# Scan stage of a three-layer network on one core: 32x32 blocks of two chunks inverted at once, every second row on a partition, transfers in two pieces instead of four

## The chip, the cores and the metric

The kernel runs on one core of one Trainium2 chip. The metric is the device time of one execution in microseconds, the median of several runs. One launch computes the whole network; its weights and inputs lie in the chip's memory in float32.

## What is computed

The network has a gated linear recurrence layer, an RWKV-7 layer and an S5 layer, for 1024 tokens of width 1024. The change lies in the RWKV-7 layer's scan, which has 16 heads of 64 channels and, in the reference, goes token by token:

```python
def step(S, inp):
    r_t, w_t, k_t, v_t, a_t, b_t = inp
    sa = jnp.einsum('bhvk,bhk->bhv', S, a_t)
    S = S * w_t[:, :, None, :] + sa[..., None] * b_t[:, :, None, :] + v_t[..., None] * k_t[:, :, None, :]
    y = jnp.einsum('bhvk,bhk->bhv', S, r_t)
    return S, y
```

The kernel does it in 16 chunks of 64 tokens. Inside a chunk, the tokens depend on each other through a 64x64 lower triangular matrix per head, and what the state receives needs the inverse of it (unit diagonal).

## The kernel before

`rwkv_scan` writes the scan as coroutines. Each yields, ahead of every piece of work, the engine that does it, a guessed duration and the events that it waits for. `weave_` takes those coroutines, together with the ones of the dense part (`rwkv_dense`: the projections of the layer) and of the output projection (`rwkv_out`), and lays down one fixed order for each engine: at each step it takes the piece that can start first by its guesses. On the chip each engine then goes through its own list in order. So a piece that stands late in a list runs late, whatever is free.

The dense part comes in four segments of 256 tokens, so four chunks can be scanned after each segment. For chunk c the scan does:

- `load_q` brings the tile QT (three buffers, `NAM` = 3; the load for chunk c waits until chunk c-3 is done, event `("y", c - 3, ..)`). `inner` multiplies it with BK (one buffer, reloaded for the second half of the heads) and DVE masks the products into AM (L1146; three buffers too).
- `diagonal` stores the two 32x32 diagonal blocks of each head to memory (abD, L1166), and `blocks` loads them into GB (L1175) as 32 (head, block) pairs on 32 partitions. It does so four times, once for each group of 32 partitions.
- `inverse` inverts all 32 blocks of the chunk by substitution on DVE: 31 steps, each a multiplication into TB (L1188) and an addition into YB (L1191) that needs it. Group e of 32 partitions holds rows e, e+4, e+8, ... of the inverse, so a step s works on s//4+1 rows of 31-s columns. YB starts as a copy of `eye`. Two chunks are in work at once, in two buffers of GB and YB; the last two chunks have buffers of their own.
- `inverted` stores YB (yiD, L1199) and `whole` loads it into YF (L1210), transposes on DVE (XT, L1215) and computes the off-diagonal block with two small matmuls (L1221, L1231) and copies on ACT (WL, YF).
- `turned` turns V and BK by TensorE; `chain` makes R from AM, QT and the state (L1286, L1289, ACT copy), multiplies it with the inverse YF (L1297; ACT copies it to UV, L1300), and updates the state St (L1306, DVE). The next chunk's `chain` needs that state.
- `outs` makes the chunk's output y (L1329, L1333; ACT copies it to PY, L1336, which sets the event `("y", c, h)`), and `post` normalizes it (L1346 with `cen`, L1477 and L1483 on psq), and `outputs` stores it to outD (event `("out", c)`).

`rwkv_out` multiplies outD with a weight matrix for tokens 0 to 511 and, as its second part, 512 to 767. Its matmuls read the tiles XO, which its coroutine `operands` makes from loads of outD (XR, L1418). It loads three tiles ahead of the one that it splits, in one sequence through both parts. The first part waits for `("out", 7)` and the end of the dense part, the second for `("out", 11)`:

```python
ks = [(y, k) for y in range(len(parts)) for k in range(KD)]
for x in range(len(ks) + nr):
    if x < len(ks):
        (y, k), (t0, n, wait) = ks[x], parts[ks[x][0]]
        yield E("S", 1, 1.46 * n / HT, wait=(list(wait) if k == 0 else []) + ...
```

Of the kernel before, what the change touches and what calls it, by code (L numbers as in the profile page):

```python
# [11 lines left out]
ALU = mybir.AluOpType  # L12
PSUM = bass.MemoryType.PSUM

P = 128
# [9 lines left out]
ILAT = 0.13  # L25
# [31 lines left out]
class Net:  # L57
# [1025 lines left out]
    def rwkv_scan(self):  # L1083

        nc, E = self.nc, self.step
        ch3 = lambda t: t.rearrange("p (c t) -> p c t", t=64)
        rsl = [slice(0, 64), slice(64, 128)]
        NC = 16
# [3 lines left out]
        two = lambda tag, shape, n=2: [self.tiny(f"{tag}{i}", shape, 1) for i in range(n)]  # L1092

        NT, NG = NC - TAIL[0], NC - TAIL[1]

        def slots(tag, shape, n, N, zero=False):
            first = dict(enumerate(two(tag, shape, n))) if tag != "AM" else {}
            last = {}
            for x in first.values() if zero else ():
                nc.gpsimd.memset(x, 0.0)  # L1100

            def get(c):
                if c < N:
                    if c % n not in first:
                        first[c] = self.tiny(f"{tag}{c}", shape, 1)
                    return first[c % n]
                if c not in last:
                    last[c] = self.rtop.tile(list(shape), F32, tag=f"{tag}t{c}", name=self.n(tag), bufs=1)
                    if zero:
                        nc.gpsimd.memset(last[c], 0.0)  # L1110
                return last[c]

            return get

        YF = slots("YF", (P, 8, 64), 2, NG, True)
        QT, AM = slots("QT", (P, 8, 2, 64), NAM, NT), slots("AM", (P, 8, 2, 2, 64), NAM, NT)
        G, Y = slots("GB", (P, 32, 32), 2, NG), slots("YB", (P, 8, 32), 2, NG)
        UV, BT, PY = two("UV", (P, 8, 2, 64)), two("BT", (P, 8, 2, 64), 1), two("PY", (P, HT))
        own = lambda c: ["rtop"] if c >= min(NT, NG) else []

        eye = self.tiny("eye", (P, 8, 32), 1)
        nc.gpsimd.memset(eye, 0.0)
        for e in range(4):
            r = eye[32 * e : 32 * e + 32]
            nc.gpsimd.affine_select(out=r, in_=r, compare_op=ALU.not_equal, fill=1.0, base=-e,
                                    pattern=[[-4, 8], [1, 32]], channel_multiplier=0)
        mask = self.msk.rearrange("p a b -> p (a b)").unsqueeze(1).to_broadcast([P, 4, 128])
        D, O = {}, {}

# [21 lines left out]
        def load_bk():  # L1151
            for x in range(2 * NC):
                c, j0 = x // 2, x % 2 * 4
                yield E("S", 1, 0.73, wait=ready(c, j0, j0 + 4) + ([("bf", x - NBK)] if x >= NBK else []), sig=[("bk", x)], par=True)
                BK[x] = self.tiny("BK", (P, 4, 2, 64), NBK)
                nc.sync.dma_start(BK[x], self.bkD[c][:, j0 : j0 + 4])
# [12 lines left out]

        def blocks():  # L1170
            for c in range(NC):
                yield E("S", 4, 1.46, wait=[("ab", c)] + ([("sub", c - 2)] if 2 <= c < NG else own(c)), sig=[("in", c)], par=True)
                src = D.pop(c).rearrange("h x j s t -> (h x j) s t")
                for e in range(4):
                    nc.sync.dma_start(G(c)[32 * e : 32 * e + 32], src)  # L1175

        def inverse(q):

            for c in range(q, NG, 2) if q < 2 else [q]:
                yield E("G", 0.97, wait=[("in", c)] + ([("yd", c - 2)] if 2 <= c < NG else own(c)))  # L1180
                g, y = G(c), Y(c)
                nc.gpsimd.tensor_copy(y, eye)
                for s in range(31):
                    nj, n = s // 4 + 1, 31 - s
                    us = 0.07 + nj * n / 960
                    yield E("V", us, lat=ILAT)
                    w = self.tiny(f"TB{q % 4}", (P, 80), 2)[:, 0 : nj * n].rearrange("p (j t) -> p j t", t=n)
                    nc.vector.tensor_mul(w, y[:, 0:nj, s : s + 1].to_broadcast([P, nj, n]),  # L1188
                                         g[:, s : s + 1, s + 1 :].to_broadcast([P, nj, n]))
                    yield E("V", us, lat=ILAT, sig=[("sub", c)] if s == 30 else ())  # L1190
                    nc.vector.tensor_add(y[:, 0:nj, s + 1 :], y[:, 0:nj, s + 1 :], w)  # L1191

        def inverted():
            for c in range(NC):
                yield E("S", 4, 0.73, wait=[("sub", c)], sig=[("yd", c)], par=True)
                yD = self.dram.tile([2, 2, 8, 32, 32], F32, name=self.n("yiD"))
                ye = yD.rearrange("h x j (k e) t -> e (h x j) k t", e=4)
                for e in range(4):
                    nc.sync.dma_start(ye[e], Y(c)[32 * e : 32 * e + 32])  # L1199
                D[c, 1] = yD  # L1200

        def whole():
# [67 lines left out]
        def chain(h):  # L1270

            js = slice(4 * h, 4 * h + 4)
            Eb = lambda e: self.EdA[:, js, e : e + 1].to_broadcast([P, 4, 64])
            state = lambda: self.tiny(f"St{h}", (P, 4, 64), 3)
            for c in range(NC):
                am, bt, uv, qz, yf = AM(c), BT[0], UV[c % 2], QT(c), YF(c)
                first = c == 0
                s = st[h][c]
                if c and c % per == 0:
                    yield E("V", 0.32, wait=ready(c))  # L1280
                    nc.vector.tensor_mul(s, s, Eb(5 * (c // per) + 4))
# [12 lines left out]
                u = ch3(ch)[:, 4:8]  # L1294
                for x in range(4):
                    for rs in rsl:
                        nc.tensor.matmul(u[rs, x], yf[rs, 4 * h + x], R[rs, x], start=True, stop=True)  # L1297
                yield E("A", 0.52)
                for hd, rs in enumerate(rsl):
                    nc.scalar.copy(uv[rs, js, 1 - hd, :], u[rs])  # L1300
                if c + 1 < NC:
                    yield E("P", 0.62, wait=[("bt", c, h)], use=0.8)
                    sp = ch3(ch)[:, 0:4]
                    for x in range(4):
                        for hd, rs in enumerate(rsl):
                            nc.tensor.matmul(sp[rs, x], bt[:, 4 * h + x, hd, :], uv[:, 4 * h + x, hd, :],  # L1306
                                             start=True, stop=True)
                    n, e = None, 5 * (c // per) + c % per
                    if not first:
                        yield E("V", 0.34, rel=ch)  # L1310
                        n = self.tiny(f"R{h}", (P, 4, 64), 1)
                        nc.vector.tensor_add(n, sp, s)
                    yield E("V", 0.32, rel=ch if first else None, wait=[("y", c - 2, h)] if c >= 2 else [],
                            sig=[("S", c, h)])
                    st[h][c + 1] = state()
                    nc.vector.tensor_mul(st[h][c + 1], sp if first else n, Eb(e))
                else:
                    yield E("P", 0.0, rel=ch, sig=[("S", c, h)])
# [54 lines left out]
        def outputs():  # L1373
            for c in range(NC):
                yield E("S", 1, 1.46, wait=[("o", c)], sig=[("out", c)], par=True)
                nc.sync.dma_start(self.outD[:, :, 64 * c : 64 * c + 64].rearrange("j p t -> p j t"), O[c % 2])

        return ([chain(0), chain(1), outs(0), outs(1), whole(), [inverse(q) for q in [0, 1, *range(NG, NC)]], blocks(), turned(), [inner(), load_bk()], diagonal(),
                 inverted(), load_q(), post(), outputs()])

    def reopen(self, wait, sig, right):
# [952 lines left out]
```

## Time and profile before

| | us |
|---|---|
| median of 3 runs | 4096.43 (4092.74 to 4096.48) |
| the profiled execution's own time | 4097.04 |
| its span, first to last instruction | 4095.0 |
| busy in the span: PE / DVE / ACT / POOL | 3826.3 / 2530.0 / 1472.3 / 184.2 |

PE is TensorE's matmuls, PEld its weight loads, DVE VectorE, ACT ScalarE, POOL GpSimd, SP the engine that issues most transfers. A time "at 2111 us" is counted from the start of the span. The RWKV-7 stage that the change touches runs from about 1300 to 2303 us; the scan of the first chunk begins at about 1550 us.

### The profile page before, as it was taken

How to read it: one execution, taken by the hardware profiler on the slowest of the kernel's cores; microseconds unless marked ns; L12 is line 12 of the kernel's file. 1: busy time of each engine (PE TensorE's matmuls, PEld its weight loads, DVE VectorE, ACT ScalarE, POOL GpSimd, SP SyncE). 2: the span in 40 equal slices, each digit the busy share in tenths (PEclk: the TensorE clock that was granted, in tenths of full speed). 3: DMA queues.
4: the chain of work that ended last, by engine and by line, in shares of the span. 5: the costliest groups of instructions: out<-in, count | busy, mean ns of one | idle time of the engine just before them, and what ended most of it. 6: DMA issues, size and time to landing. Idle time of an engine off the chain costs nothing.

```text
span 4095.0 us, 57944 instructions
## 1 busy us (share of the span) xinstructions
PE 3826.3 (93%) x22238; PEld 3151.6 (77%) x22238; DVE 2530.0 (62%) x5213; ACT 1472.3 (36%) x2507; POOL 184.2 (4%) x374
## 2 busy tenths in 40 slices
PE   7998999999999888898979699999999999999899
PEld 6776788888877778787867677888887787888687
DVE  6565733333363688788766584444437699997655
ACT  5456411111132675555543321121114323323523
POOL 0000000000000010000010010011100000000000
PEclk8999999999999899999989799999999999999999
DMA  3111111111122699678776522121212244343775
GB/s 110 47 44 44 56 42 52 42 57 42 45 63 80 203 256 253 171 212 213 205 201 180 151 75 66 44 68 52 72 36 63 75 127 117 107 121 102 234 226 190
DMA packets 688548, 464.97 MB, mean 114 GB/s; under 512 B 189652, under 2 KB 609424, under 8 KB 688272
## 3 DMA queue, kind: packets, MB, share of 16 engines
q1 hardware_dynamic: 515376, 370.42, 30.7%
q10 hardware_dynamic: 167552, 81.80, 7.1%
q0 software_dynamic: 5344, 9.05, 0.7%
q8 instruction: 175, 2.87, 0.3%
q14 instruction: 101, 0.83, 0.1%
HBM read 355.11 MB, written 107.22 MB: 113 GB/s over the span
## 4 chain that ended last, share of the span: by engine, by line
PE 62%; DVE 16%; DMA 8%; issue 7%; ACT 5%; POOL 1%; SPq 1%; ACTq 0%; DVEq 0%; POOLq 0%
PE mm L249 14%; PE mm L251 14%; PE mm L250 13%; PE ob L249 4%; PE ob L250 4%; PE ob L251 4%; DVE cy L1928 4%; DMA wraw<-in_rw_w_rkv_dram 1%; DVE w L881 1%; PE mm L2119 1%; DVE w L216 1%; PE mm L2118 1%; PE mm L2117 1%; DMA GB<-abD 1%; DVE TB L1188 1%
## 5 line engine op out<-in xcount | busy, mean ns | idle before, releaser
L249 PE MATMUL mm<-T,w 128*128 128x512 f32 (+1 forms) x2944 | 1152.2, 393 | 49.6 <-ACT w L215 26.7
L251 PE MATMUL mm<-T,w 128*128 128x512 f32 (+1 forms) x2944 | 1148.0, 391 | 4.6 <-DVE w L216 4.6
L250 PE MATMUL mm<-T,w 128*128 128x512 f32 (+1 forms) x2944 | 1149.9, 391 | 1.0 <-DVE T L1426 0.9
L249 PEld LDWEIGHTS mm<-T,w 128*128 128x128 f32 x2944 | 558.3, 190 | 176.2 <-ACT w L215 31.0
L251 PEld LDWEIGHTS mm<-T,w 128*128 128x128 f32 x2944 | 558.5, 190 | 121.5 <-DVE w L216 6.4
L250 PEld LDWEIGHTS mm<-T,w 128*128 128x128 f32 x2944 | 559.2, 190 | 116.0 <-DVE T L1426 1.6
L215 ACT CAST w<-wraw 128x1024 fp32r<-128x1024 f32 (+1 forms) x286 | 288.3, 1015 | 991.8 <-PE mm L250 695.5
L216 DVE TENSOR_TENSOR w<-wraw,w 128x1024 fp32r<-128x1024 f32 (+1 forms) x286 | 335.1, 1177 | 373.4 <-ACT w L215 371.4
L396 DVE TENSOR_TENSOR h<-ob,h 128x512 f32<-128x512 f32 x416 | 286.3, 690 | 233.5 <-PE ob L251 230.1
L249 PE MATMUL ob<-S,w 128*128 128x512 f32 x896 | 360.3, 402 | 22.1 <-DVE h L396 21.2
L1928 DVE SCALAR_TENSOR_TENSOR cy<-cu,pv,cy 128x512 f32<-128x512 f32 x480 | 350.8, 748 | 12.3 <-ACT cy L1926 2.6
L251 PE MATMUL ob<-S,w 128*128 128x512 f32 x896 | 355.6, 397 | 0.0
L250 PE MATMUL ob<-S,w 128*128 128x512 f32 x896 | 355.2, 396 | 0.0
L249 PE MATMUL mm<-M,w 128*128 128x256 f32 x768 | 259.5, 338 | 18.9 <-ACT M L855 11.0
L250 PE MATMUL mm<-N,w 128*128 128x256 f32 x768 | 229.7, 299 | 12.2 <-DVE N L857 12.2
L251 PE MATMUL mm<-M,w 128*128 128x256 f32 x768 | 229.6, 299 | 5.7 <-DVE w L881 5.4
L249 PEld LDWEIGHTS ob<-S,w 128*128 128x128 f32 x896 | 170.3, 190 | 71.3 <-DVE h L396 30.6
L251 PEld LDWEIGHTS ob<-S,w 128*128 128x128 f32 x896 | 170.3, 190 | 39.0
L250 PEld LDWEIGHTS ob<-S,w 128*128 128x128 f32 x896 | 170.6, 190 | 36.4 <-DVE S L216 0.4
L446 DVE TENSOR_TENSOR S<-mm,S 128x512 f32<-128x512 f32 x88 | 60.8, 691 | 211.2 <-PE mm L251 209.4
L249 PEld LDWEIGHTS mm<-M,w 128*128 128x128 f32 x768 | 156.3, 204 | 32.2 <-ACT M L855 14.7
L215 ACT CAST S<-S 128x512 fp32r<-128x512 f32 x128 | 79.3, 620 | 267.9 <-DVE S L446 157.4
(467 smaller groups left out, 5253.3 us busy)
## 6 DMA issues: line engine op xcount, KB each, us to landing
wraw<-in_rw_w_rkv_dram ACTq DMA_DIRECT2D x96, 512.0 KB
wraw<-in_ffn_w_in_dram SPq DMA_DIRECT2D x88, 512.0 KB
wraw<-in_w_in_dram SPq DMA_DIRECT2D x48, 512.0 KB
wraw<-in_ffn_w_out_dram SPq DMA_DIRECT2D x44, 512.0 KB
BK<-bkD SPq DMA_DIRECT2D x64, 256.0 KB
wraw<-in_rw_w_o_dram ACTq DMA_DIRECT2D x24, 512.0 KB
wraw<-in_lru_w_in_dram SPq DMA_DIRECT2D x20, 512.0 KB
wraw<-in_ple_w_gate_dram SPq DMA_DIRECT2D x16, 512.0 KB
```

Source lines behind the costliest of these rows:

```text
L215: self.nc.scalar.copy(hi, x)
L216: self.nc.vector.tensor_sub(lo, x, hi.bitcast(F32))
L249: nc.tensor.matmul(ps, w[0], x[0], start=first, stop=False)
L250: nc.tensor.matmul(ps, w[0], x[1], start=False, stop=False)
L251: nc.tensor.matmul(ps, w[1], x[0], start=False, stop=last)
L396: nc.vector.tensor_add(h[m][half], ps, h[m][half])
L446: nc.vector.tensor_mul(a, ps, sg.pop((b, j, half)))
L881: nc.vector.tensor_sub(wl.rearrange(fl), r.rearrange(fl), wh.bitcast(F32).rearrange(fl))
L1188: nc.vector.tensor_mul(w, y[:, 0:nj, s : s + 1].to_broadcast([P, nj, n]), g[:, s : s + 1, s + 1 :].to_broadcast([P, nj, n]))
L1928: nc.vector.scalar_tensor_tensor(y, x[:, k : k + HT], cw(k), y, ALU.mult, ALU.add)
L2117: nc.tensor.matmul(ps, a[0], w[0], start=k == 0, stop=False)
L2118: nc.tensor.matmul(ps, a[0], w[1], start=False, stop=False)
```

## The change

The blocks of two chunks, 2b and 2b+1, now share one buffer of GB and one of YB and are inverted together. Two groups of 64 partitions hold the even and the odd rows; in each group the first 32 partitions belong to the even chunk, the other 32 to the odd one. A step works on s//2+1 rows. Each transfer that had four pieces for a chunk has two (GB, yiD). There is no `eye` any more: POOL clears YB and sets its ones, and no longer waits for the blocks' arrival; the first multiplication does. The special buffers of the last two chunks are gone, and `inverse` is run by two coroutines, for even and odd pairs.

```diff
-        G, Y = slots("GB", (P, 32, 32), 2, NG), slots("YB", (P, 8, 32), 2, NG)
+
+        G, Y = two("GB", (P, 32, 32)), two("YB", (P, 16, 32))
...
-        eye = self.tiny("eye", (P, 8, 32), 1)
-        nc.gpsimd.memset(eye, 0.0)
...
         def blocks():
             for c in range(NC):
-                yield E("S", 4, 1.46, wait=[("ab", c)] + ([("sub", c - 2)] if 2 <= c < NG else own(c)), sig=[("in", c)], par=True)
+                yield E("S", 2, 0.98, wait=[("ab", c)] + ([("sub", c // 2 - 2)] if c >= 4 else []), sig=[("in", c)], par=True)
                 src = D.pop(c).rearrange("h x j s t -> (h x j) s t")
-                for e in range(4):
-                    nc.sync.dma_start(G(c)[32 * e : 32 * e + 32], src)
+                for r0 in (0, 64):
+                    r0 += 32 * (c % 2)
+                    nc.sync.dma_start(G[c // 2 % 2][r0 : r0 + 32], src)
...
-            for c in range(q, NG, 2) if q < 2 else [q]:
-                yield E("G", 0.97, wait=[("in", c)] + ([("yd", c - 2)] if 2 <= c < NG else own(c)))
-                g, y = G(c), Y(c)
-                nc.gpsimd.tensor_copy(y, eye)
+            for b in range(q, NC // 2, 2):
+                yield E("G", 0.97, wait=[("yd", c) for c in (2 * b - 4, 2 * b - 3) if c >= 0])
+                g, y = G[q], Y[q]
+                nc.gpsimd.memset(y, 0.0)
+                for e in range(2):
+                    nc.gpsimd.memset(y[64 * e : 64 * e + 64].rearrange("p a b -> p (a b)")[:, e:512:34], 1.0)
                 for s in range(31):
-                    nj, n = s // 4 + 1, 31 - s
+                    nj, n = s // 2 + 1, 31 - s
                     us = 0.07 + nj * n / 960
-                    yield E("V", us, lat=ILAT)
+                    yield E("V", us, lat=ILAT, wait=() if s else [("in", 2 * b), ("in", 2 * b + 1)])
...
-                    yield E("V", us, lat=ILAT, sig=[("sub", c)] if s == 30 else ())
+                    yield E("V", us, lat=ILAT, sig=[("sub", b)] if s == 30 else ())
...
-                yield E("S", 4, 0.73, wait=[("sub", c)], sig=[("yd", c)], par=True)
+                yield E("S", 2, 0.73, wait=[("sub", c // 2)], sig=[("yd", c)], par=True)
...
-                for e in range(4):
-                    nc.sync.dma_start(ye[e], Y(c)[32 * e : 32 * e + 32])
+                for e in range(2):
+                    r0 = 64 * e + 32 * (c % 2)
+                    nc.sync.dma_start(ye[e], Y[c // 2 % 2][r0 : r0 + 32])
```

Since `weave_` lays all lists down anew, the change moves much that the diff does not show. Two places matter. (From about L1190 on, the changed file's line numbers are lower by 2.)

**PE, around the end of the dense part.** The last dense instruction on PE is the last matmul with `bo` (L1059). Before, there stand around it the end of chunk 11 (y, then `post`), the first products of chunk 12 (g from QT and BK), and at once the first output projection (XO, 512 wide):

```order
L1483 MATMUL g_19593<-ident,psq_19588 128x128 x4
L1059 MATMUL g_19602<-L_19269,bo 128x256
L1329 MATMUL y_19610<-QT_8729,St_19263 64x64 x8
L1333 MATMUL y_19610<-AM_11730,UV_8735 64x64 x8
...
L1346 MATMUL g_19672<-PY_8738,cen 128x512
L1477 MATMUL g_19686<-bsel,psq_19683 128x2 x4
L1248 MATMUL g_19694<-ident,V_19663 64x64 x16
L1141 MATMUL g_19724<-QT_8727,BK_19188 128x128
...
L1483 MATMUL g_19740<-ident,psq_19734 128x128 x4
L249 MATMUL mm_19757<-XO_19751,w_19691 128x512
L250 MATMUL mm_19757<-XO_19752,w_19691 128x512
L251 MATMUL mm_19757<-XO_19751,w_19692 128x512
```

Now the last dense instruction is followed by the off-diagonal block of chunk 6 (g from XT and AM), its product with the inverse (ch from R and YF), the state update (ch from UV and BT), and chunk 7:

```order
L1475 MATMUL g_17409<-bsel,F_17368 128x2 x2
L1481 MATMUL g_17419<-ident,F_17368 128x128 x2
L1059 MATMUL g_17441<-L_17284,bo 128x256
L1219 MATMUL g_17497<-XT_17494,AM_8741 32x32 x16
L1229 MATMUL g_17517<-YF_8723,WL_17498 32x32 x16
L1295 MATMUL ch_16652<-R_16697,YF_8723 64x64 x8
...
L1304 MATMUL ch_16652<-UV_8734,BT_8736 64x64 x8
...
L1219 MATMUL g_17583<-XT_17568,AM_11466 32x32 x16
L1256 MATMUL g_17605<-ident,BK_16978 128x128 x4
L1284 MATMUL ch_17612<-UV_8735,AM_11466 64x64 x2
L1287 MATMUL ch_17612<-St_17581,QT_8728 64x64 x2
```

Counted over the whole list, so many chunks have a piece behind the last dense instruction:

| piece | before | now |
|---|---|---|
| off-diagonal block (XT, WL) and product with the inverse | 4 | 10 |
| state update | 3 | 9 |
| R (ch from UV and AM, and from St and QT), BK turned | 4 | 9 |
| y, `post` (cen, psq) | 5 | 10 |
| V turned | 4 | 8 |
| products of QT and BK for AM | 4 | 7 |

From that instruction to the off-diagonal block of chunk 12, 330 rows on, the list holds scan work alone but for 15 XO matmuls ahead of chunk 8 and 27 just ahead of chunk 12. In that stretch the products for chunks 9, 11 and 13 stand behind the y of chunks 6, 8 and 10 each, and each pair's blocks (W of 8 and 9, of 10 and 11, of 12 and 13) stand behind those products.

**SP, the loads of the output projection's operands.** Before, the first eight loads (512 wide) and the first four of the second part (256 wide) follow each other with one store of a chunk's output (outD, chunk 11) between them:

```order
L1376 DMA outD<-psq_19650 128x8x64
...
L1418 DMA XR_19675<-outD 128x512
L1418 DMA XR_19677<-outD 128x512
...
L1376 DMA outD<-psq_19754 128x8x64
L1418 DMA XR_19764<-outD 128x512
L1418 DMA XR_19773<-outD 128x512
...
L1418 DMA XR_19798<-outD 128x512
...
L1418 DMA XR_19865<-outD 128x256
L1418 DMA XR_19876<-outD 128x256
```

Now they lie apart. The stores of chunks 7, 8, 9, 10 and 11 are rows 558, 584, 592, 609 and 616 of the list, the 512-wide loads rows 559 to 570, and the first 256-wide load is row 619:

```order
L1374 DMA outD<-psq_18076 128x8x64
L1416 DMA XR_18114<-outD 128x512
...
L1197 DMA yiD_18129<-YB_8732 512x1x32 x2
...
L1416 DMA XR_18155<-outD 128x512
...
L1457 DMA HO_18178<-hD 128x512
L1208 DMA YF_8723<-yiD_18129 32x8x32 x4
L1416 DMA XR_18191<-outD 128x512
...
L1208 DMA YF_8724<-yiD_18132 32x8x32 x4
...
L1374 DMA outD<-psq_18630 128x8x64
...
L1374 DMA outD<-psq_19423 128x8x64
L1197 DMA yiD_19455<-YB_8732 512x1x32 x2
...
L1416 DMA XR_19461<-outD 128x256
```

Since `operands` makes an XO tile three loads late and its ninth load waits for `("out", 11)`, five of the first eight tiles are made ahead of chunk 11's output, and the rest behind it.

## Rows read from the trace of the kernel before

**Rows 1.** The page, its first line.

```profile
span 4095.0 us, 57944 instructions
```

**Rows 2.** Busy time by stretch (us), with clock and DMA share.

```profile
core 0: us, PE busy (x) PEld busy (x) DVE busy (x) ACT busy (x) POOL busy (x), PEclk, DMA share, GB/s
1495.00:2111.00 616.00, 543.77 (x6208) 468.73 (x6209) 476.37 (x1543) 356.60 (x813) 49.37 (x120) 0.93 0.76 206
2111.00:2303.00 192.00, 153.58 (x1826) 126.86 (x1822) 112.76 (x374) 64.04 (x122) 16.30 (x22) 0.89 0.64 184
```

**Rows 3.** Waits of PE, 1495 to 2111 us: total, times, longest.

```profile
PE mm L250 <- DVE N L857: 10.1, 7, 4.2
...
PE mm L251 <- DVE w L881: 4.1, 9, 0.8
```

**Rows 4.** Waits of PE, 2111 to 2303 us.

```profile
PE g L1221 <- DVE XT L1215: 12.2, 1, 12.2
```

**Rows 5.** Timeline of PE, 2108 to 2112 us: start, length, instruction.

```profile
2110.26 0.60 PE L1059 MATMUL g<-L,bo 128*128 128x256 f32 x2
```

**Rows 6.** Groups of DVE instructions, 1570 to 2275 us.

```profile
L1188 DVE TENSOR_TENSOR TB<-YB,GB 128x60 f32<-128x60 f32 (+22 forms) x496 | 95.8, 207 | 19.1 <-DMA GB<-abD 5.0 <-POOL YB L1182 4.3 <-issue 2.7
...
L1053 DVE TENSOR_TENSOR L<-L,F 128x256 f32<-128x256 f32 x24 | 10.0, 418 | 3.9 <-ACT F L1049 3.8
```

**Rows 7.** By stretch, for tiles ch, BK, y, psq, V, cen, XT.

```profile
1495.00:2303.00 808.00, 79.05 (x1984) 68.28 (x1984) 12.45 (x30) 35.34 (x96) 0.92 0.73 201
1495.00:2303.00 808.00, 62.07 (x640) 50.04 (x640) 0.92 0.73 201
1495.00:2303.00 808.00, 41.92 (x992) 35.44 (x992) 0.00 (x0) 11.87 (x32) 0.92 0.73 201
1495.00:2303.00 808.00, 36.41 (x256) 34.15 (x256) 11.02 (x16) 19.37 (x32) 0.92 0.73 201
1495.00:2303.00 808.00, 19.20 (x512) 17.07 (x512) 0.92 0.73 201
1495.00:2303.00 808.00, 17.28 (x32) 4.89 (x32) 0.00 (x0) 0.92 0.73 201
1495.00:2303.00 808.00, 12.44 (x512) 10.42 (x512) 13.89 (x32) 0.92 0.73 201
```

**Rows 8.** Timeline of DVE around the inverses of chunks 11 and 15.

```profile
2002.35 1.28 DVE L1146 TENSOR_TENSOR AM<-g,msk 128x512 f32<-128x512 f32 x2
...
2235.23 1.29 DVE L1146 TENSOR_TENSOR AM<-g,msk 128x512 f32<-128x512 f32 x2 [2.95 <-PE g L1141]
...
2246.59 0.19 DVE L1188 TENSOR_TENSOR TB<-YB,GB 128x31 f32<-128x31 f32 x1
...
2254.98 0.24 DVE L1188 TENSOR_TENSOR TB<-YB,GB 128x76 f32<-128x76 f32 x1
...
2255.25 0.24 DVE L1191 TENSOR_TENSOR YB<-YB,TB 128x76 f32<-128x76 f32 x1
...
2272.10 0.17 DVE L1191 TENSOR_TENSOR YB<-YB,TB 128x8 f32<-128x8 f32 x1
...
2281.57 0.90 DVE L1215 STREAM_TRANSPOSE XT<-YF 32x256 f32<-32x256 f32 x2
```

**Rows 9.** Timeline of ACT: chunks 6, 8, 12 and 15.

```profile
1942.20 1.56 ACT L1300 COPY UV<-ch 64x256 f32<-64x256 f32 x4 [1.18 <-DVE YB L1191]
...
1951.63 0.37 ACT L1336 COPY PY<-y 128x256 f32<-128x256 f32 x1 [0.54 <-PE y L1333]
...
1986.94 0.37 ACT L1336 COPY PY<-y 128x256 f32<-128x256 f32 x1
...
2211.96 0.36 ACT L1336 COPY PY<-y 128x256 f32<-128x256 f32 x1
...
2287.51 1.60 ACT L1300 COPY UV<-ch 64x256 f32<-64x256 f32 x4 [0.17 <-PE ch L1297]
...
2292.04 0.37 ACT L1336 COPY PY<-y 128x256 f32<-128x256 f32 x1 [1.40 <-PE y L1333]
```

More of the change, by code (lines that the diff above doesn't have):

```diff
@@ L1116, in rwkv_scan @@
         QT, AM = slots("QT", (P, 8, 2, 64), NAM, NT), slots("AM", (P, 8, 2, 2, 64), NAM, NT)
-        G, Y = slots("GB", (P, 32, 32), 2, NG), slots("YB", (P, 8, 32), 2, NG)
+        G, Y = two("GB", (P, 32, 32)), two("YB", (P, 16, 32))
         UV, BT, PY = two("UV", (P, 8, 2, 64)), two("BT", (P, 8, 2, 64), 1), two("PY", (P, HT))
         own = lambda c: ["rtop"] if c >= min(NT, NG) else []
-        eye = self.tiny("eye", (P, 8, 32), 1)
-        nc.gpsimd.memset(eye, 0.0)
-        for e in range(4):
-            r = eye[32 * e : 32 * e + 32]
-            nc.gpsimd.affine_select(out=r, in_=r, compare_op=ALU.not_equal, fill=1.0, base=-e,
-                                    pattern=[[-4, 8], [1, 32]], channel_multiplier=0)
         mask = self.msk.rearrange("p a b -> p (a b)").unsqueeze(1).to_broadcast([P, 4, 128])
@@ L1171, in blocks @@
             for c in range(NC):
-                yield E("S", 4, 1.46, wait=[("ab", c)] + ([("sub", c - 2)] if 2 <= c < NG else own(c)), sig=[("in", c)], par=True)
+                yield E("S", 2, 0.98, wait=[("ab", c)] + ([("sub", c // 2 - 2)] if c >= 4 else []), sig=[("in", c)], par=True)
                 src = D.pop(c).rearrange("h x j s t -> (h x j) s t")
-                for e in range(4):
-                    nc.sync.dma_start(G(c)[32 * e : 32 * e + 32], src)
+                for r0 in (0, 64):
+                    r0 += 32 * (c % 2)
+                    nc.sync.dma_start(G[c // 2 % 2][r0 : r0 + 32], src)
         def inverse(q):
-            for c in range(q, NG, 2) if q < 2 else [q]:
-                yield E("G", 0.97, wait=[("in", c)] + ([("yd", c - 2)] if 2 <= c < NG else own(c)))
-                g, y = G(c), Y(c)
-                nc.gpsimd.tensor_copy(y, eye)
+            for b in range(q, NC // 2, 2):
[4 more added lines that the diff above has]
+                    nc.gpsimd.memset(y[64 * e : 64 * e + 64].rearrange("p a b -> p (a b)")[:, e:512:34], 1.0)
                 for s in range(31):
-                    nj, n = s // 4 + 1, 31 - s
+                    nj, n = s // 2 + 1, 31 - s
                     us = 0.07 + nj * n / 960
-                    yield E("V", us, lat=ILAT)
-                    w = self.tiny(f"TB{q % 4}", (P, 80), 2)[:, 0 : nj * n].rearrange("p (j t) -> p j t", t=n)
+                    yield E("V", us, lat=ILAT, wait=() if s else [("in", 2 * b), ("in", 2 * b + 1)])
+                    w = self.tiny(f"TB{q}", (P, 136), 1)[:, 0 : nj * n].rearrange("p (j t) -> p j t", t=n)
                     nc.vector.tensor_mul(w, y[:, 0:nj, s : s + 1].to_broadcast([P, nj, n]),
                                          g[:, s : s + 1, s + 1 :].to_broadcast([P, nj, n]))
-                    yield E("V", us, lat=ILAT, sig=[("sub", c)] if s == 30 else ())
+                    yield E("V", us, lat=ILAT, sig=[("sub", b)] if s == 30 else ())
                     nc.vector.tensor_add(y[:, 0:nj, s + 1 :], y[:, 0:nj, s + 1 :], w)
@@ L1194, in inverted @@
             for c in range(NC):
-                yield E("S", 4, 0.73, wait=[("sub", c)], sig=[("yd", c)], par=True)
+                yield E("S", 2, 0.73, wait=[("sub", c // 2)], sig=[("yd", c)], par=True)
                 yD = self.dram.tile([2, 2, 8, 32, 32], F32, name=self.n("yiD"))
-                ye = yD.rearrange("h x j (k e) t -> e (h x j) k t", e=4)
-                for e in range(4):
-                    nc.sync.dma_start(ye[e], Y(c)[32 * e : 32 * e + 32])
+                ye = yD.rearrange("h x j (k e) t -> e (h x j) k t", e=2)
+                for e in range(2):
+                    r0 = 64 * e + 32 * (c % 2)
+                    nc.sync.dma_start(ye[e], Y[c // 2 % 2][r0 : r0 + 32])
                 D[c, 1] = yD
@@ L1376, in outputs @@
                 nc.sync.dma_start(self.outD[:, :, 64 * c : 64 * c + 64].rearrange("j p t -> p j t"), O[c % 2])
-        return ([chain(0), chain(1), outs(0), outs(1), whole(), [inverse(q) for q in [0, 1, *range(NG, NC)]], blocks(), turned(), [inner(), load_bk()], diagonal(),
+        return ([chain(0), chain(1), outs(0), outs(1), whole(), [inverse(q) for q in range(2)], blocks(), turned(), [inner(), load_bk()], diagonal(),
                  inverted(), load_q(), post(), outputs()])
```

## The prediction

> **What bounds the kernel now.** The page gives the span, 4095.0 us [rows 1]; the execution's own time is 4097.04 us, 2.04 us more, and the median of three runs is 4096.43 us, 0.6 us below it. I make the sum against 4097. The change touches only the RWKV-7 stage, so I read that stage alone, first by busy time. I cut it at 2111 us, because there the dense part's last matmul ends (2110.26 + 0.60 us, [rows 5]). From 1495 us to there PE is busy 543.77 of 616 us, 88.3%, and DVE 476.37 us, 77% [rows 2]. From 2111 to 2303 us PE is busy 153.58 of 192 us. So PE is nearly full while dense work lasts, and the reader should look at the rest. In the dense stretch, the longest waits of PE for DVE are 10.1 and 4.1 us, both for dense operands [rows 3]. Behind it stands one wait of 12.2 us, for the last chunk's inverse [rows 4]. PE therefore sets the time as long as its list holds work that doesn't wait, and the scan's chain sets it where that work has run out.
>
> **The change, step by step.** *DVE.* There were 992 inverse instructions (496 in each line), of 207 ns on the mean [rows 6]; there are 496 now. By the code a chunk had 3,120 columns in 62 instructions, 50 in each; a pair has 5,712 in 62, 92 in each. The new sizes reach 136 columns and no row shows those. An instruction of 76 columns takes 0.24 us [rows 8] and one of 256 columns 0.418 us [rows 6]. These are the bounds, and 92 lies near the first: 0.24 + 16 x 0.178/180 = 0.256 us. Each waits for the one before, and successive starts at 76 columns lie 0.27 us apart, 0.03 us more than the duration [rows 8]. So a pair needs 62 x 0.286 = 17.7 us where nothing comes between. In sum of durations DVE saves 205 - 127 = 78 us.
>
> What is that worth? [...]
>
> The trace speaks against such a gain: PE waits little for DVE. What counts is where the instructions stand now.
>
> *Work moved behind the dense part.* Ten chunks instead of four have their inverse applied behind the last dense instruction. I price it by the busy time of each tile's matmuls in 808 us, over 16 chunks [rows 7]: ch 79.05 us, BK 62.07, y 41.92, psq 36.41, V 19.20, cen 17.28 and XT 12.44 (WL, with as many matmuls of the same size, taken as XT). For a chunk that is 4.94, 3.88, 2.62, 2.28, 1.20, 1.08 and 2 x 0.78 us, 17.6 in all. By the counts in the section on the change, the moved parts are ch 5.5 chunks, 27.2 us; BK 3.4 (136 of the 640 matmuls), 13.2; y, psq and cen 5 each, 29.9; V 4, 4.8; XT and WL 6, 9.3. Together 84.4 us. Taken out of a stretch that is busy 88.3%, the dense part ends 95.6 us earlier, at 2015 us. Bounds: if PE ran that stretch without a gap, 84 us (2027 us); if the saved DVE time also took PE's two waits away, 14 us more (2001 us).
>
> *The cycle of a pair.* With three buffers of AM and QT, chunk 2p+3 can't be prepared before chunk 2p has its y. The pair (2p+2, 2p+3) is inverted only when both of its chunks are there. So y of an even chunk waits, through a whole chain, for y of the even chunk before it. Before, a chunk's inverse needed its own products alone. The chain, from rows of before:
>
> - end of PY to the end of AM three chunks on: 1986.94 + 0.37 [rows 9] to 2002.35 + 1.28 [rows 8], 16.3 us (QT's load, products, BK's reload).
> - end of AM to the first inverse instruction: 2235.23 + 1.29 to 2246.59, 10.1 us [rows 8]. Two loads of GB and POOL's copy fall out of it; I take 8.6.
> - the inverse: 17.7 us. The next chunk's AM (two rows of 1.28 us) and about 2.2 us of `post` stand between its instructions in DVE's list, and I allow 1.5 us for waiting on them: 24 us.
> - its last instruction to XT (stored, loaded): 2272.27 to 2281.57, 9.3 us [rows 8]; 9 with two issues fewer of twice the pieces.
> - XT to UV: 2281.57 to 2287.51, 5.9 us [rows 8, 9].
> - UV to the end of PY: 1942.20 to 1952.00, 9.8 us [rows 9].
>
> That is 73.6 us. Low end 62: first link 10, the inverse 19, the last 8.5. High end 82: PE idles and its granted clock falls, as in the stretch at 0.89 [rows 2], and DVE waits in the inverse for products that come late. One check: end of PY of chunk 12 to end of PY of chunk 15, the same chain for one chunk in the busy tail, took 2212.32 to 2292.41, 80.1 us [rows 9].
>
> In such a cycle PE's list holds two chunks, 35 us. Before, the output projection's 384 matmuls filled what was left. Now `operands` waits for chunk 11's output, so that only 15 of them stand in the first three cycles. That is the cover which is gone.
>
> *The sum.* The dense part ends at 2015 us. 14 inverse instructions are then left on DVE (4 us); with 9 to XT and 5.9 to UV, chunk 6 has UV 19 us on, and PY at 2015 + 19 + 9.8 = 2044. Three cycles, to chunk 12: 221 us, 2265. The fourth, to chunk 14, has output projection between its steps; as in the check, 80 us, 2345. Then come chunk 15's y, about 5 us, the last 75 projection matmuls, and `post`. Before, 2303 - 2292.4 = 11 us followed the last PY; with the projection between, I take 25 us, to 2370. The stage ended at 2303, so it grows by 67 us: 4097 + 67 = 4164 us. Less work in four GB pieces and no POOL hop are in the links above; `eye` and the two special buffers cost nothing either way, since POOL is busy 65.7 of 808 us [rows 2].
>
> **The rivals.**
>
> *The chain is short, or covered (faster).* The place is the three cycles. If nothing waited there, they would hold PE's own work, 105 us instead of 221, and the kernel would take 4048 us. It decides at a cycle of 73.6 - 67/3 = 51 us; below that the change gains. For it: DVE is nearly empty there, the loads of the tail are alone on the queue, and the last chunk's wait of 12.2 us [rows 4] is covered by 75 projection matmuls now. Against: 51 us is 11 below the sum of my low ends.
>
> *DVE's relief is what counts (faster).* If the lists' new order cost nothing and PE merely lost its waits for DVE, 10.1 + 4.1 + 12.2 us [rows 3, 4], the kernel would take 4071 us. For it: DVE is busy 77% in the dense stretch. Against: the counts above, by which the order does change. [...]
>
> *No change.* The cycle is 51 us give or take 3, or the dense part ends near 1990 us and the cycle is 60: 4089 to 4105 us.
>
> *The dense part doesn't end earlier by so much (slower still).* Its loads are then squeezed: transfer share 0.76 over 616 us [rows 2] must go into some 520 us, less what the moved chunks load. If the dense part gained only half, it would end at 2063 us, and the kernel would take 4212 us. For it: the share is high. Against: PE's longest waits listed there are for DVE and short, and a share of 0.85 is below full.
>
> **How the numbers follow.** My forecast, a chain that sets the pace after an earlier dense end, gets 0.74. It holds 4115 (cycle 62, dense end 2001) to 4200. The slower rival gets 0.14, the short chain 0.05, DVE's relief 0.02, no change 0.05. The likeliest is 4164 us. The range 4113 to 4216 leaves out both faster rivals, no change and some of the slower one's upper side. A difference of 0.2%, 8 us, is about what a measurement of this kernel can tell from none. Faster than that: 0.07; within it: 0.05; slower: 0.88.
>
> **What would show it.** In the changed kernel's profile the last L1059 should end near 2015 us (2001 to 2063). From there to chunk 12 PE's busy share should be about half, with three near-equal cycles of 62 to 82 us between the y of chunks 6, 8, 10 and 12, and PE's waits should name XT, R or BK's and QT's loads. The inverse of a pair should take some 24 us there, and its instructions 0.25 us on the mean. The stage should end near 2370 us. I am wrong if the cycles take under 55 us, if dense matmuls still stand beside chunks 8 to 11, or if the time before 1500 us or after the stage moves.

## The result, and the profile after

The changed kernel takes 4154.22 us, the median of 4 runs (4149.41 to 4158.41), against 4094.59 us for the kernel before beside it: ratio 1.0140, 95% interval 1.0114 to 1.0166. The profiled execution took 4157.12 us, 60.1 us more than the one before.

The first lines of the page, which answer to [rows 1]: DVE's busy time fell (2530.0 us before), and PE's rose a little (3826.3).

```profile
span 4155.4 us, 57369 instructions
...
PE 3837.6 (92%) x22238; PEld 3159.4 (76%) x22238; DVE 2492.4 (60%) x4717; ACT 1472.9 (35%) x2507; POOL 180.9 (4%) x377
```

Busy time by stretch, with the columns of [rows 2], cut at the new dense end, at the y of chunk 12 and at the stage's end:

```profile
1495.00:2009.00 514.00, 452.60 (x4404) 391.52 (x4400) 378.16 (x953) 309.31 (x701) 37.20 (x110) 0.92 0.77 214
2009.00:2237.00 228.00, 146.90 (x2438) 120.24 (x2439) 108.18 (x313) 64.19 (x141) 12.25 (x15) 0.74 0.46 127
2237.00:2362.00 125.00, 103.17 (x1151) 86.20 (x1150) 62.03 (x143) 45.18 (x84) 12.44 (x17) 0.88 0.54 160
```

The first stretch is as full as before: 88.1% for PE, at nearly the same clock and transfer share. It ends 102 us earlier. The second is new: for 228 us PE is busy 64% and no engine is full; the granted clock of TensorE is 0.74 there on the mean (1.00 from 2036 to 2050 us, 0.50 from 2064 to 2082). The last dense matmul and PE's longest waits in the second and the third stretch answer to [rows 5, 3, 4]:

```profile
2007.63 1.22 PE L1059 MATMUL g<-L,bo 128*128 128x256 f32 x2 [3.13 <-DVE L L1057]
```

```profile
PE g L1219 <- DVE XT L1213: 27.9, 5, 13.9
PE mm L249 <- ACT XO L1422: 15.7, 2, 11.8
...
PE g L1135 <- DMA QT<-qD: 7.5, 6, 2.5
```

```profile
PE ms L273 <- DVE L L313: 12.9, 1, 12.9
```

PE waits for the inverses (XT) five times, and for the output projection's tiles where these stand ahead of scan work. The wait in the third stretch, of PE for the next norm (L313), has grown as well: it was 0.8 us before.

The second cycle, from the y of chunk 8 to that of chunk 10, from the timelines of ACT and DVE (compare [rows 8, 9]):

```profile
2106.60 0.37 ACT L1334 COPY PY<-y 128x256 f32<-128x256 f32 x1 [0.49 <-PE y L1331]
...
2160.48 1.60 ACT L1298 COPY UV<-ch 64x256 f32<-64x256 f32 x4 [1.22 <-PE ch L1295]
...
2170.41 0.37 ACT L1334 COPY PY<-y 128x256 f32<-128x256 f32 x1 [0.49 <-PE y L1331]
```

```profile
2115.78 1.29 DVE L1140 TENSOR_TENSOR AM<-g,msk 128x512 f32<-128x512 f32 x2 [1.75 <-PE g L1135]
...
2126.02 0.19 DVE L1185 TENSOR_TENSOR TB<-YB,GB 128x31 f32<-128x31 f32 x1 [1.74 <-DMA GB<-abD]
...
2149.15 0.19 DVE L1188 TENSOR_TENSOR YB<-YB,TB 128x16 f32<-128x16 f32 x1
2154.05 0.44 DVE L1213 STREAM_TRANSPOSE XT<-YF 32x256 f32<-32x256 f32 x1 [4.71 <-DMA YF<-yiD]
```

Read in order of time, this is one chain: y of chunk 8 ends at 2106.97, AM of chunk 11 at 2117.07, the pair's inverse runs from 2126.02 to 2149.34, XT starts at 2154.05, UV at 2160.48, y of chunk 10 ends at 2170.78. The links are 10.1, 8.9, 23.3, 4.7, 6.4 and 10.3 us, 63.8 in all.

### The profile page after: what moved, and what is told of

Same layout as the page of the kernel before. It is cut to its first block, busy times and chain, and to the rows that moved or that the text cites. A ratio compares the mean times of both kernels' runs of the same rounds, so it can differ in the third digit from the quotient of the medians.

```text
span 4155.4 us, 57369 instructions
## 1 busy us (share of the span) xinstructions
PE 3837.6 (92%) x22238; PEld 3159.4 (76%) x22238; DVE 2492.4 (60%) x4717; ACT 1472.9 (35%) x2507; POOL 180.9 (4%) x377
## 4 chain that ended last, share of the span: by engine, by line
PE 65%; DVE 15%; DMA 8%; issue 5%; ACT 5%; POOL 1%; SPq 1%; ACTq 0%; DVEq 0%; POOLq 0%
PE mm L249 14%; PE mm L251 14%; PE mm L250 14%; PE ob L249 4%; PE ob L250 4%; PE ob L251 4%; DVE cy L1926 3%; DVE w L881 1%; DMA wraw<-in_rw_w_rkv_dram 1%; DMA BK<-bkD 1%; PE g L1135 1%; DVE w L216 1%; PE g L1481 1%; DVE YB L1188 1%; PE mm L2117 1%
```

## The experiments

Three theories stood at the start. Theory 1 is the prediction's: a pair can be inverted only when the third AM buffer has come free for its second chunk, so pairs follow each other in one chain, and the planner (`weave_`) leaves ten chunks of it behind the dense part. Theory 2: the price lies in the new form itself (instructions twice as wide, transfers in two pieces), wherever it stands. Theory 3 is that only the output projection's cover is missing.

The table holds what the sections below compare: chunks whose off-diagonal block (L1219, before L1221; the W of the expectations) stands in PE's list behind the last dense instruction, when that instruction (last L1059) starts, and the time between the ends of PY of chunks 6, 8, 10, 12 and 14 in the profiled execution (`-` where they are not compared). Ratios are to the kernel before, beside each run. A pair is named by its even chunk: pair 10 is chunks 10 and 11.

| kernel | median us | ratio, 95% | chunks behind | last L1059 | pair cycles us |
|---|---|---|---|---|---|
| before | 4094.59 | 1 | 4 | 2110.5 | - |
| the change | 4154.22 | 1.0114 to 1.0166 | 10 | 2008.2 | 72.5, 63.8, 66.5, 83.8 |
| alone | 4119.96 | 1.0028 to 1.0064 | 7 | 2059.7 | - |
| wait_both | 4204.74 | 1.0229 to 1.0281 | 10 | 2027.8 | 82, 71, 76, 91 |
| filler | 4162.54 | 1.0116 to 1.0178 | 10 | 2016.4 | 81, 78, 72, 79 |
| half_inverse | 4144.46 | 1.0078 to 1.0140 | 10 | 2006.2 | 69, 61, 73, 84 |
| stores_on_pool | 4156.69 | 1.0114 to 1.0165 | 10 | 2006.0 | 69, 65, 75, 90 |
| half_stores_on_pool | 4141.06 | 1.0074 to 1.0129 | 10 | 2003.3 | 68, 60, 72, 86 |
| half_replanned | 4087.86 | 0.9956 to 0.9992 | 7 | 2031.3 | -, 59, 58, 77 |
| small_pieces | 4148.49 | 1.0097 to 1.0165 | 6 | 2120.6 | -, 95, 70, 84 |
| four_am | 4106.86 | 1.0012 to 1.0041 | 4 | 2119.1 | -, -, -, 33 |
| alone_am4 | 4135.62 | 1.0081 to 1.0134 | 4 | 2147.5 | - |
| four_am_one | 4091.15 | 0.9977 to 1.0005 | 4 | 2090.5 | -, -, -, 33 |
| four_am_one_eleven | 4095.23 | 0.9979 to 1.0011 | 5 | 2097.0 | -, -, -, 34 |

### The wait and the form, apart: alone, wait_both

alone is the changed kernel with one chunk at a time on 64 partitions; wait_both is the kernel before, in which the planner lets a chunk's inverse wait for the blocks of both chunks and so places it behind them in the lists:

```diff
-            for b in range(q, NC // 2, 2):
-                yield E("G", 0.97, wait=[("yd", c) for c in (2 * b - 4, 2 * b - 3) if c >= 0])
-                g, y = G[q], Y[q]
+            for c in range(q, NC, 2):
+                yield E("G", 0.97, wait=[("yd", c - 2)] if c >= 2 else ())
+                g, y = G[q][0:64], Y[q][0:64]
```

```diff
-                yield E("G", 0.97, wait=[("in", c)] + ([("yd", c - 2)] if 2 <= c < NG else own(c)))
+                yield E("G", 0.97, wait=[("in", c), ("in", c ^ 1)] + ([("yd", c - 2)] if 2 <= c < NG else own(c)))
```

> The change's layout and its two-piece transfers, but one chunk at a time, on 64 partitions; a chunk's inverse waits for its own blocks alone, and all 992 instructions are there, at 92 columns. Theory 1 (the pair waits for its second chunk, which under three AM buffers waits for the y of the pair before; that cycle sets the time): most of the loss goes, 4090 to 4125 us; what stays is the larger DVE work. Theory 2 (the layout: longer DVE instructions and fewer, larger transfers make each link of the chain longer): no better than the changed kernel, 4140 to 4170 us.

> The kernel before, with its layout, its four-piece transfers and one chunk at a time, but the planner places a chunk's inverse behind the arrival of both chunks' blocks. Theory 1: as slow as the changed kernel, 4135 to 4170 us, since ten chunks again stand behind the dense part. Theory 2: as fast as before, 4085 to 4105 us.

alone, the change's form without its wait, is 0.5% slower than before, within theory 1's range; from what its 25 us come is not separated. wait_both, the wait without the form, is 2.6% slower, above theory 1's range of 4135 to 4170: the wait alone costs 110 us, and the rest of the change then wins 50 us back. So theory 2 is out for the bulk. In the profiled executions that gain lies in the four cycles, which are 7 to 10 us shorter each in the change than in wait_both, 33 us together, and ahead of them: the y of chunk 6 ends at 2034.5 us in the change and at 2057.6 in wait_both.

### The missing cover: filler

The changed kernel, in which `operands` loads ahead within a part and not across the two, so that the first part's tiles don't wait for chunk 11:

```diff
+            todo = []
+            for y in range(len(parts)):
+                todo += [("load", KD * y + k) for k in range(nr - 1)]
+                for k in range(KD):
+                    todo += [("load", KD * y + k + nr - 1)] if k + nr - 1 < KD else []
+                    todo += [("split", KD * y + k)]
```

> The changed kernel, but the output projection splits all tiles of its first part without a load of the second part ahead of them, so 192 of its matmuls can stand in the three cycles behind the dense part. Theory 1: the cycles stay, PE only idles less in them and the stage's end gets shorter; 4120 to 4150 us. Theory 3 (the missing cover alone is the loss): back to 4090 to 4110 us.

No gain: the time is that of the change, above theory 1's range too, and theory 3 falls. In the first three cycles PE is busy 176.52 of 231 us, 76%, where the change has 133.26 of 202.8, 66%. filler's row, then the change's:

```profile
2043.00:2274.00 231.00, 176.52 (x2315) 140.44 (x2317) 119.82 (x314) 70.18 (x140) 11.50 (x12) 0.81 0.55 157
```

```profile
2034.50:2237.30 202.80, 133.26 (x2103) 108.11 (x2098) 100.94 (x288) 57.45 (x123) 11.48 (x12) 0.76 0.49 136
```

But these cycles grow by 29 us together, and the y of chunk 6 comes 8 us later; the fourth cycle and the stage's end get 20 us shorter. 270 projection matmuls now stand among the scan work of the three cycles in PE's list, ahead of pieces of the chain. (filler's profiled execution took 4178.07 us, 15.5 us more than its median, so the 29 us are rather too many.) Whether projection matmuls that stand only in the chain's gaps would gain is not shown.

### What the inverse is worth: half_inverse, stores_on_pool, half_stores_on_pool, half_replanned

half_inverse leaves out steps 16 to 30 and keeps the lists as they were:

```diff
+                    if s >= 16:
+                        yield E("V", us, lat=ILAT, sig=[("sub", b)] if s == 30 else ())
+                        continue
```

> The changed kernel with the last 15 of the 31 steps of each inverse left out (the inverse is wrong), all engines' lists otherwise the same. Theory 1: each pair's inverse is 30 x 0.28 = 8.5 us shorter, and behind the dense part four or five of them lie on the chain one after the other: 34 to 42 us less than the changed kernel, 4110 to 4122 us. Theory 3, or a chain that runs past the inverse: 4145 to 4158 us.

A miss: 10 us, not 34 to 42. The chain had become shorter, but its next link did not start. For pair 10 the last instruction of the inverse in half_inverse, and SP's queue behind it:

```profile
2131.53 0.29 DVE L1191 TENSOR_TENSOR YB<-YB,TB 128x128 f32<-128x128 f32 x1
```

```profile
2136.81 0.34 SPq L1344 DMA_DIRECT2D gb<-gbD  x1
2137.19 0.43 SPq L1377 DMA_DIRECT2D outD<-psq  x1
2137.67 3.54 SPq L1200 DMA_DIRECT2D yiD<-YB  x4
```

so yiD stood behind a load and a store of the odd chunk before, 6 us late. In the four cycles it left 13.1, 5.9, 7.6 and 18.1 us after the inverse's end, in the change 1.7, 0.1, 0.1 and 3.4. I took the store for the cause and moved it, and the loads XR that wait for such stores, to POOL, with the whole inverse as control:

```diff
-                nc.sync.dma_start(self.outD[:, :, 64 * c : 64 * c + 64].rearrange("j p t -> p j t"), O[c % 2])
+                nc.gpsimd.dma_start(self.outD[:, :, 64 * c : 64 * c + 64].rearrange("j p t -> p j t"), O[c % 2])
...
-                    nc.sync.dma_start(raw[x], self.outD[k][:, t0 : t0 + n])
+                    nc.gpsimd.dma_start(raw[x], self.outD[k][:, t0 : t0 + n])
```

> The changed kernel with the stores to outD and the loads XR that wait for them issued by POOL in place of SP, all else as it was. In the changed kernel's trace the store yiD follows the end of the inverse directly (yiD(10) at 2149.4, the inverse's end at 2149.3), so both theories expect little: 4135 to 4160 us.

> half_inverse (the last 15 of the 31 steps of each inverse left out) with the same stores and loads moved from SP to POOL. Theory 1a (the saving of half_inverse was caught by SP's list, in which yiD stands behind the store outD of an odd chunk and the loads XR that wait for outD): cycles of a pair of 50 to 60 us, 4105 to 4130 us, at least 15 under half_inverse's 4144.5. Theory 1b (the chain of the state through the odd chunks, and not SP's list, is as long as the inverse's chain): 4135 to 4150 us, as half_inverse.

The control is as expected; the other is 1b's number, not 1a's. But its trace shows a neighbour in the same place. The inverse's last instruction and SP's queue:

```profile
2120.70 0.29 DVE L1191 TENSOR_TENSOR YB<-YB,TB 128x128 f32<-128x128 f32 x1
```

```profile
2125.98 0.34 SPq L1344 DMA_DIRECT2D gb<-gbD  x1
2126.41 3.52 SPq L1200 DMA_DIRECT2D yiD<-YB  x4
```

The load gb left at 2125.98 us, just behind the last instruction in which `post` of the chunk before reads its buffer (psq from PY and gb, to 2125.95), and yiD stands behind it, 5.4 us late (6.7, 5.4, 6.7 and 13.8 us in the four cycles). So half_replanned let the planner write the lists for the short inverse:

```diff
-                for s in range(31):
+                for s in range(16):
```

> The changed kernel with the last 15 of the 31 steps of each inverse left out, as in half_inverse and half_stores_on_pool, but here the planner knows of it and writes the lists anew (in half_stores_on_pool yiD of pair 10 still stood on SP behind the load gb of the next chunk, 2126.41 us against the inverse's end at 2121.0, and yiD of pair 14 behind the loads HO, 2276.91 against 2263.1). 7 chunks' W stand behind the last dense instruction, against 10. Theory 1a (the halved inverse's saving was caught by entries of SP's list, written for the whole inverse): yiD within 2 us of the inverse's end, cycles of a pair under 60 us, 4095 to 4120 us. Theory 1b (another chain of the same length bounds the pairs): 4130 to 4150 us.

Here yiD leaves with the inverse, 0.1 us after its end in each of the four pairs, and the chain runs at 58 to 59 us a cycle up to chunk 12 (the fourth cycle takes 77). For pair 10:

```profile
2136.73 0.29 DVE L1188 TENSOR_TENSOR YB<-YB,TB 128x128 f32<-128x128 f32 x1
```

```profile
2137.08 2.58 SPq L1197 DMA_DIRECT2D yiD<-YB  x4
```

This fits 1a: the entries of SP's list that were written for the whole inverse caught the saving. But the planner wrote all engines' lists anew, so that SP's list alone did it is not shown. The time, 4087.86 us, is below what I expected, 4095 to 4120: three chunks fewer stand behind the dense part, too. Half an inverse is worth 66 us when the lists are written for it (some of it through those three chunks), and 10 when they aren't.

### The buffer: small_pieces, four_am, alone_am4, four_am_one, four_am_one_eleven

The kernel with a fourth AM and QT buffer, four_am, also has NMP = 8 in place of 13, so small_pieces, with NMP = 8 alone, is its control.

four_am has both edits:

```diff
-NAM = 3
+NAM = 4
...
-NMP = 13
+NMP = 8
```

> A control: the changed kernel with NMP 8 in place of 13 (how many of the dense products' operand tiles the planner may hold prepared ahead), which frees the memory that the next kernel needs and changes the planner's order: 6 chunks' W stand behind the last dense instruction on PE, where the changed kernel has 10. Theory 1 (what costs is the number of pair cycles that stand behind the dense products, since a pair's diagonal blocks need the third AM buffer of the pair before) expects less than the changed kernel's 4154 us: one or two cycles fewer in the open, 4120 to 4145. Theory 2 (the two-chunk inverse with its two-piece transfers costs the same wherever it stands) expects 4145 to 4165.

> The control small_pieces with NAM 4 in place of 3, so that the pair's second chunk finds a free AM buffer and need not wait for the pair before; 4 chunks' W stand behind the last dense instruction, as in the kernel before. Theory 1: at least 20 us under small_pieces, 4090 to 4120 us, and cycles of a pair under 62 us. Theory 2: within 10 us of small_pieces.

small_pieces is a miss for theory 1: 4148.49 us lies in theory 2's range, 6 us under the change though four chunks fewer stand behind the dense part. The dense part ends 112 us later there. Of the cycles, the one of 95 us has dense work beside it for 57 us, and the two behind it, 70 and 84 us, are about as long as the change's 66.5 and 83.8. What the smaller NMP costs apart from the new order was not separated.

four_am is theory 1's clear case: 42 us under its control with the same form of inverse. NAM counts the buffers of AM and of QT, so it shows the two together. The inverse of pair 14 no longer waits for the y of chunk 12, which ends at 2239.2 us; it starts while that of pair 12 is in its last steps. Its first instruction (in a row with one of pair 12) and its last:

```profile
2202.61 0.33 DVE L1185 TENSOR_TENSOR TB<-YB,GB 128x31 f32<-128x31 f32 x2
...
2229.41 0.19 DVE L1188 TENSOR_TENSOR YB<-YB,TB 128x16 f32<-128x16 f32 x1
```

In small_pieces the y of chunk 12 ends at 2229.3 us and that inverse starts at 2254.3. Both dense parts end at about 2120 us; four_am has two chunks more inside its own, and its stage ends 37 us earlier. Busy time from the dense part's end to the stage's end, of small_pieces and then of four_am:

```profile
2121.20:2353.30 232.10, 179.47 (x2237) 146.31 (x2236) 114.39 (x287) 75.75 (x148) 15.63 (x21) 0.81 0.55 159
```

```profile
2119.70:2316.10 196.40, 150.81 (x1744) 124.11 (x1744) 98.27 (x242) 64.60 (x119) 11.09 (x15) 0.83 0.61 180
```

PE has 29 us less to do there and idles 7 us less. Between the y of chunks 12 and 14 lie 33 us where small_pieces has 84, but these two aren't the same work: 219 projection matmuls stand in the longer one and 54 in the shorter, and PE is 93% and 97% busy. So the 51 us between them are mostly matmuls that stand elsewhere, and no measure of the wait. ACT's timeline of four_am, and behind it that of small_pieces:

```profile
2238.79 0.37 ACT L1334 COPY PY<-y 128x256 f32<-128x256 f32 x1
...
2271.68 0.37 ACT L1334 COPY PY<-y 128x256 f32<-128x256 f32 x1 [0.59 <-PE y L1331]
```

```profile
2228.96 0.37 ACT L1334 COPY PY<-y 128x256 f32<-128x256 f32 x1 [0.54 <-PE y L1331]
...
2313.16 0.37 ACT L1334 COPY PY<-y 128x256 f32<-128x256 f32 x1 [0.31 <-PE y L1331]
```

> alone (the change's layout and two-piece transfers, one chunk at a time on 64 partitions) with NAM 4 and NMP 8 as in four_am. 4 chunks' W stand behind the last dense instruction. Theory 1 (with a free fourth AM buffer the two-chunk wait costs little, so that the two-chunk inverse, which halves DVE's instructions, wins): slower than four_am's 4106.9 us, 4105 to 4130. Theory 2 (the two-chunk inverse is a loss even with four buffers): faster than four_am, 4085 to 4102 us.

With four buffers and NMP 8 the pair's inverse is better than that of one chunk on 64 partitions: alone_am4 is 29 us slower than four_am, a little more than theory 1 expected, and its dense part ends 28 us later. Against the kernel before's own form, one chunk on 128 partitions with four-piece transfers, the pair was not tried with four buffers, so which of these two is better there stays open. alone_am4 is also 16 us slower than alone, though it has a buffer more, so in that form the smaller NMP, or the order that the planner made with it, costs more than the buffer gains.

Last came a version with four buffers of AM and QT, one of GB, YB and TB, and NMP 10 in place of 8:

```diff
-        G, Y = two("GB", (P, 32, 32)), two("YB", (P, 16, 32))
+        G, Y = two("GB", (P, 32, 32), 1), two("YB", (P, 16, 32), 1)
```

> four_am with one GB, one YB and one TB buffer in place of two (pairs of inverses one after the other, never two at a time), which frees 6 KB on a partition, so that NMP is 10 and not 8. 4 chunks' W behind the last dense instruction, and at least 195 of the 384 XO products stand ahead of the last two pairs' W. Theory 1 (what remained against the kernel before in four_am, 11 us, is the smaller NMP and the late XO products, not the two-chunk wait): 4080 to 4103 us. The rival (a second pair of buffers lets one pair's inverse run beside the other's, and giving it up costs what it costs in waiting): 4105 to 4130.

> four_am_one with NMP 11 in place of 10: 5 chunks' W stand behind the last dense instruction. If NMP is worth something by itself this is 0 to 10 us under four_am_one; if the number of cycles behind the dense products decides, it is 5 to 20 us above it.

four_am_one came out as theory 1 expected, 16 us under four_am, and can't be told from the kernel before. It has fewer inverse buffers, a larger NMP and a new order at once, so which of them made the 16 us is not separated. NMP 11 can't be told from NMP 10, so whether NMP has a price of its own stays open here. No version here that does the whole inverse beats the kernel before by more than the measurement can tell; half_replanned does, without half of the steps.

## Why the prediction was right, step by step

- *The dense part's end.* 2015 us forecast; 2008.85 measured, 102 us earlier than before where the sum gave 95.6. About 4 of these 6 us are not the change's: long ahead of the stage its profiled execution is already so much in front of the one before (the first `ob` matmul starts at 102.3 us, before at 106.6). So the sum by counts was 2 to 3 us too small, inside its bounds.
- *The pair's inverse.* 24 us forecast; 22.7, 23.3, 25.1 in the first three cycles. The mean instruction took 253 ns (0.256 forecast):

```profile
L1185 DVE TENSOR_TENSOR TB<-YB,GB 128x126 f32<-128x126 f32 (+22 forms) x248 | 62.8, 253 | 13.8 <-DMA GB<-abD 8.6
L1188 DVE TENSOR_TENSOR YB<-YB,TB 128x126 f32<-128x126 f32 (+22 forms) x248 | 62.6, 253 | 5.3
```

- *The cycle.* The mechanism held: wait_both makes such cycles without the new form, and in four_am, with a fourth buffer, the inverse no longer waits for the y of the pair before. The size was 73.6 us; the three measured 67.6 on the mean. Two links were too long: y to AM, 16.3 us, was 9.3, 10.1 and 8.8 (it was read in a stretch in which PE had other work; in the fourth cycle, where PE has such work again, it took 18.4), and the inverse's end to XT, 9 us, was 4.7 in the second cycle and 7.2 in the third. The first cycle has 17.2 there for another reason, for which the sum had no term. Loads of the projection stand on SP ahead of yiD and between yiD and YF, and the four pieces of yiD took 7.55 us to issue (2.57 in the second cycle); what they waited for is not shown:

```profile
2074.21 1.75 SPq L1416 DMA_DIRECT2D XR<-outD  x4
2076.07 7.55 SPq L1197 DMA_DIRECT2D yiD<-YB  x4
2083.71 1.52 SPq L1416 DMA_DIRECT2D XR<-outD  x3
2085.29 0.42 SPq L1457 DMA_DIRECT2D HO<-hD  x1
2085.80 1.86 SPq L1208 DMA_DIRECT2D YF<-yiD  x4
```

- *The cover that is gone.* The count was wrong: 71 projection matmuls ran in the three cycles, not 15. The first had 15, the second none, the third 56. By the order shown in the section on the change 27 more stand just ahead of the block of chunk 12, and so inside the third cycle. PE's busy share was 66% where about half was forecast. The meaning is not borne out either: filler put 270 matmuls there and gained nothing; cover that is placed better was not tried.
- *The clock.* The forecast's high end had a falling clock in it. The granted clock did fall, to 0.72, 0.71 and 0.85 in the three cycles. In the second one the two links from XT to the end of PY, 6.4 and 10.3 us, are 0.5 us each above the rows of before; the clock was 0.50 in both for the first link, and 0.82 against 1.00 before for the second. No run separates its price.
- *The fourth cycle and the end.* 80 us forecast, 83.8 measured. Here PE is busy 94%, with 217 projection matmuls among the scan work, so PE's list and not the chain alone sets the time:

```profile
2237.30:2321.10 83.80, 78.73 (x910) 64.07 (x909) 46.59 (x114) 30.00 (x56) 5.42 (x6) 0.92 0.56 167
```

Behind the y of chunk 14, which ended at 2321.06, I took 25 us to the stage's end; the chain of waits shows 40 to the end of L273. Chunk 15's y took 9.4 us (5 forecast), and its `cen` matmul came 8 us after that, behind projection matmuls in PE's list. Then seven of the eight loads of h stand on SP behind the last chunk's store, and the next norm waits for them:

```profile
2348.49 0.23 SPq L1374
...
2349.94 4.35 DMA h<-hD
...
2358.16 0.70 DVE L L313
...
2358.91 1.88 PE ms L273 x8
```

- *The sum.* The cycles were 18 us too long, chunk 6 came 10 us earlier than forecast (2034.5 against 2044), the fourth cycle and the end were 4 and 15 us too short. The errors cancel to 10 us: 4164 forecast, 4154 measured. That it came so near is in part luck; what held is the mechanism of three chained cycles beside a PE that isn't full. Behind the stage little changed: the last L281 of the program starts 58.0 us later.
- *The rivals.* The short chain would have needed 51 us a cycle; even with half an inverse, in half_replanned, it took 58. What the change gains apart from the wait is real (50 us between wait_both and the change) and smaller than what the wait costs; how much of it is DVE's relief and how much the transfers' is not separated. The slower rival's dense end of 2063 us did not come: the first stretch kept its transfer share, 0.77 against 0.76. The argument against it was read from rows that leave out PE's longest wait of that stretch, 10.6 us in four times for BK's loads.

## What to carry to other kernels

Joining two pieces of work makes the later of the two set the start (wait_both, which has that wait alone, is 110 us slower than before); before doing it, count the buffers that the later one needs, and whose release frees them (with a fourth buffer, four_am is 42 us under its control). Where every engine follows a written list, look at what stands ahead of the next step's transfer in its queue before shortening a step, and let the lists be written anew before judging what the step is worth: half an inverse gained 10 us in half_inverse, where yiD left 5.9 to 18.1 us after the inverse's end, and 66 in half_replanned, where it left 0.1 us after it (some of the 66 through three chunks fewer behind the dense part). A gap in a waiting stretch is not yet a gain to fill: in filler 270 matmuls stood in the three cycles ahead of pieces of the chain, and the kernel took 4162.54 us where the change took 4154.22.

## What was not expected of the hardware

In the kernel before, two independent chains of small DVE instructions overlapped on the engine. DVE's timeline shows two instructions of two chunks in 0.35 us together, and the next two starting 0.26 us on (a row gives the shape of its first instruction):

```profile
2008.28 0.35 DVE L1188 TENSOR_TENSOR TB<-YB,GB 128x42 f32<-128x42 f32 x2
2008.54 0.35 DVE L1191 TENSOR_TENSOR YB<-YB,TB 128x42 f32<-128x42 f32 x2
```

The first of them has 42 columns, the second 69, and they take 202 and 232 ns, so each starts while the one before it is still at work:

```profile
L1188 DVE TENSOR_TENSOR TB<-YB,GB 128x69 f32<-128x69 f32 x1 | 0.2, 232 | 0.0
...
L1188 DVE TENSOR_TENSOR TB<-YB,GB 128x42 f32<-128x42 f32 x1 | 0.2, 202 | 0.0
```

So the 992 instructions of 207 ns, 205 us in sum, kept DVE busy for only 178.80 us, by the busy time of their tile, and the 496 of after for 125.42:

```profile
1570.00:2300.00 730.00, 178.80 (x992) 0.92 0.73 198
```

```profile
1570.00:2300.00 730.00, 125.42 (x496) 0.86 0.65 181
```

The change therefore saved 53 us of DVE's time in the inverses and not the 78 of the sum; over the whole span DVE's busy time fell by 38 us, from 2530.0 to 2492.4. In wait_both two such chains together took 26 to 27 us from the first start to the last end (pairs 8 to 12), the joined one 22.7 to 25.1: joined, the chain was 1 to 4 us shorter.
